# Scaling each token row twice: one buffer per tile, filled with gaps and scaled in place, instead of separate load and output tiles

## The chip, the cores and the metric

The kernel runs on one core of a Trainium2 chip. The metric is device time in microseconds of one execution. A core has a tensor engine (PE, not used here), VectorE (DVE), ScalarE (ACT), GpSimd (POOL), a sync engine (SP) that only waits and issues, and sixteen DMA engines that move data between the chip's main memory (HBM) and the on-chip memory (SBUF, 128 partitions). A DMA is issued from an engine's queue; here SP and ACT issue all of them.

## The reference

```python
batch, seq, hidden, n_experts = 16, 1024, 512, 8      # k = 2
def reference(x, expert_indices, expert_weights):
    x_expanded = x[:, :, np.newaxis, :].repeat(k, axis=2)
    weights = expert_weights[..., np.newaxis]
    return (x_expanded * weights).astype(np.float32)
```

Every token row of 512 float32 values (2 KB) is multiplied by two scalars, and both products are stored next to each other. The expert indices are not used. There are 16,384 tokens: 33.6 MB of x and 0.13 MB of weights are read, 67.1 MB are written. Each value that is read takes part in two multiplications.

## The kernel before, in words

The tokens are laid out over the 128 partitions so that each partition owns 128 consecutive tokens (`A_TOTAL`, L25). In the memory of x, the 128 tokens of a partition are one contiguous run, and so are their output rows. All weights are loaded first, as one tile `w_tile` of 1 KB per partition (L44, on SP's queue).

The main loop (L60) runs 16 times over blocks of 8 tokens per partition. `issue_load` (L48 to L55) allots one of three x tiles (16 KB per partition) and loads it by two DMAs on ACT's queue, four tokens (8 KB per partition, 1 MB in all) each. It is called two blocks ahead of the block that is computed. The block is then computed in two halves, each into its own output tile of 16 KB per partition (`o_tile`, L66, six buffers). A half is eight multiplications of a 128x512 operand by a scalar per partition: in the first half all eight are done by ScalarE (L79), in the second half six by ScalarE, one by VectorE and one by GpSimd (L85). Each finished half is stored by one DMA of 2 MB on SP's queue (L93), 16 KB contiguous in each partition on both sides.

What sets the order: each engine runs its own instructions in program order. On ACT's queue the two load DMAs of block `it + 2` stand in front of the multiplications of block `it`, so a load is issued when ScalarE has got through the block before, and waits there if the x tile that it will overwrite is still being read. Semaphores, put in by the framework, make a multiplication wait for its load and for a free output tile, a store wait for its multiplications, and a load wait for the readers of its tile. On SP's queue the stores follow each other in order.

Of the kernel before, what the change touches and what calls it, by code (L numbers as in the profile page):

```python
# [1 line left out]

# [4 lines left out]


@with_exitstack
def kernel(  # L10
    ctx: ExitStack,
    tc: tile.TileContext,
    x: bass.AP,
    expert_indices: bass.AP,
    expert_weights: bass.AP,
    out: bass.AP,
):
    nc = tc.nc

    batch, seq, hidden = x.shape  # L20
    k = expert_weights.shape[-1]
    P = nc.NUM_PARTITIONS
    ntok = batch * seq
    assert ntok % P == 0
    A_TOTAL = ntok // P  # L25

    xr = x.rearrange("b s h -> (b s) h").rearrange("(p a) h -> p a h", a=A_TOTAL)
    outr = out.rearrange("b s k h -> (b s) (k h)").rearrange(
        "(p a) n -> p a n", a=A_TOTAL
    )  # L30
    wr = expert_weights.rearrange("b s k -> (b s) k").rearrange(
        "(p a) k -> p a k", a=A_TOTAL
    )

    A = 8
    H = A // 2
    n_iters = A_TOTAL // A

    w_pool = ctx.enter_context(tc.tile_pool(name="w_pool", bufs=1))
    x_pool = ctx.enter_context(tc.tile_pool(name="x_pool", bufs=3))  # L40
    o_pool = ctx.enter_context(tc.tile_pool(name="o_pool", bufs=6))

    w_tile = w_pool.tile([P, A_TOTAL, k], mybir.dt.float32)
    nc.sync.dma_start(out=w_tile, in_=wr)  # L44

    x_tiles = {}

    def issue_load(j):  # L48
        if j >= n_iters:
            return  # L50
        t = x_pool.tile([P, A, hidden], mybir.dt.float32)
        a0 = j * A
        nc.scalar.dma_start(out=t[:, 0:H, :], in_=xr[:, a0 : a0 + H, :])
        nc.scalar.dma_start(out=t[:, H:A, :], in_=xr[:, a0 + H : a0 + A, :])
        x_tiles[j] = t  # L55

    issue_load(0)
    issue_load(1)

    for it in range(n_iters):  # L60
        a0 = it * A
        issue_load(it + 2)
        x_tile = x_tiles.pop(it)

        for half in range(2):
            o_tile = o_pool.tile([P, H, k, hidden], mybir.dt.float32)  # L66
            base = half * H
            opc = 0
            for ai in range(base, base + H):
                for kk in range(k):  # L70
                    w_ap = w_tile[:, a0 + ai, kk : kk + 1]
                    eng = nc.scalar
                    if half == 1:
                        if opc == 0 or opc == 8:
                            eng = nc.vector
                        elif opc == 4:
                            eng = nc.gpsimd
                    if eng is nc.scalar:
                        nc.scalar.mul(  # L79
                            out=o_tile[:, ai - base, kk, :],  # L80
                            in_=x_tile[:, ai, :],
                            mul=w_ap,
                        )
                    else:
                        eng.tensor_scalar(  # L85
                            out=o_tile[:, ai - base, kk, :],
                            in0=x_tile[:, ai, :],
                            scalar1=w_ap,
                            scalar2=None,
                            op0=mybir.AluOpType.mult,  # L90
                        )
                    opc += 1
            nc.sync.dma_start(  # L93
                out=outr[:, a0 + base : a0 + base + H, :], in_=o_tile
            )


# [1 line left out]
_INS = ['x', 'expert_indices', 'expert_weights']  # L99
_OUTS = [((16, 1024, 2, 512), 'float32')]  # L100


# [23 lines left out]
```

## Time and profile before

| what | before |
|---|---|
| time, three runs | 243.03 us median (242.64 to 245.35) |
| profiled execution, from its first to its last instruction | 243.2 us |
| moved by DMA in that span | 100.82 MB, mean 415 GB/s |
| store DMAs (SP's queue) | 32 of 2 MB, median 26.1 us from issue to landing |
| load DMAs (ACT's queue) | 32 of 1 MB, median 28.8 us from issue to landing |
| ScalarE multiplications | 224, mean 710 ns |
| VectorE multiplications | 16, mean 486 ns |
| GpSimd multiplications | 16, mean 1858 ns |

The page gives no time for the profiled execution other than its span; at 243.2 us it stands 0.2 us above the median of the three runs.

How to read the views that follow: in a line of a wait, the numbers are the time waited in total, how often, and the longest one, in us; "SPq" is the sync engine's own queue, which issues the stores. In a table by stage each line is a stretch of the span, its length, the busy time of each engine in it with the number of instructions, the tensor clock, the mean busy share of the sixteen DMA engines and what they moved in GB/s. A DMA line gives packets, MB and the share of the time of sixteen engines that these packets took. A DMA is cut into packets[...].

### The profile page before, as it was taken

To read this page: it belongs to the slowest core of one execution; us is meant where nothing else is said; L and a number is where in the kernel's file an instruction comes from. 1 tells how busy PE (TensorE), PEld (TensorE's weight loads), DVE (VectorE), ACT (ScalarE), POOL (GpSimd) and SP (SyncE) were. 2 spreads that over 40 slices of the span, in tenths; PEclk is the share of its full clock that TensorE was granted. 3 is DMA by queue.
4 is the path that set the end of the run, shared out by engine and by line. 5 is a ranking of instruction groups with operands and counts; after the bars stand their busy time and mean duration, and the time that the engine had idled before them with its cause. 6 is when DMAs were issued, how large, how long until landed. Compare 5 with 4: busy or idle time off the path is not lost.

```text
span 243.2 us, 500 instructions
## 1 busy us (share of the span) xinstructions
DVE 7.8 (3%) x16; ACT 140.3 (58%) x225; POOL 29.9 (12%) x20
## 2 busy tenths in 40 slices
DVE  0000000000000000000000000000000000000000
ACT  1999863909367291864909549094580996463000
POOL 0330303002030200303003030030301103020000
DMA  7999999999999999999999999999999999999991
GB/s 263 428 358 423 435 430 426 438 422 430 438 419 435 434 418 433 430 423 437 427 426 435 422 433 434 423 431 438 423 428 437 419 428 442 420 438 433 431 431 65
DMA packets 9363, 100.82 MB, mean 415 GB/s; under 512 B 1040, under 2 KB 1168, under 8 KB 1168
## 3 DMA queue, kind: packets, MB, share of 16 engines
q1 hardware_dynamic: 4752, 67.24, 64.8%
q10 hardware_dynamic: 4608, 33.56, 33.2%
q14 instruction: 3, 0.02, 0.0%
HBM read 33.69 MB, written 67.11 MB: 414 GB/s over the span
## 4 chain that ended last, share of the span: by engine, by line
DMA 83%; ACT 3%; ACTq 0%; issue 0%
DMA t<-in_x_dram 83%; ACT o_tile L79 3%; ACTq L121 0%; ACTq L79 0%
## 5 line engine op out<-in xcount | busy, mean ns | idle before, releaser
L79 ACT ACTIVATE o_tile<-t,w_tile 128x512 f32<-128x512 f32 x224 | 139.0, 710 | 75.7 <-DMA t<-in_x_dram 74.3
L85 POOL TENSOR_SCALAR o_tile<-t,w_tile 128x512 f32<-128x512 f32 x16 | 29.7, 1858 | 189.2 <-DMA t<-in_x_dram 189.2
L85 DVE TENSOR_SCALAR o_tile<-t,w_tile 128x512 f32<-128x512 f32 x16 | 7.8, 486 | 210.2 <-DMA t<-in_x_dram 210.2
L79 ACT ACT_TABLE_LOAD x1 | 1.3, 1283 | 5.3 <-DMA w_tile<-in_expert_weights_dram 5.3
L110 POOL MEMSET const-float32-0.0<- 128x1 f32 x1 | 0.1, 99 | 0.2 <-issue 0.2
L110 POOL MEMSET const-bfloat16-1.0<- 128x1 bf16 x1 | 0.1, 102 | 0.0
L110 POOL MEMSET const-uint8-127<- 128x1 uint8 x1 | 0.1, 102 | 0.0
L110 POOL MEMSET const-float32-1.0<- 128x1 f32 x1 | 0.1, 99 | 0.0
## 6 DMA issues: line engine op xcount, KB each, us to landing
out_dram<-o_tile SPq DMA_DIRECT2D x32, 2048.0 KB, 26.1
t<-in_x_dram ACTq DMA_DIRECT2D x32, 1024.0 KB, 28.8
w_tile<-in_expert_weights_dram SPq DMA_DIRECT2D x1, 128.0 KB, 4.5
```

Of the source, the lines that this page charges most:

```text
L79: nc.scalar.mul(out=o_tile[:, ai - base, kk, :], in_=x_tile[:, ai, :], mul=w_ap,)
L85: eng.tensor_scalar(out=o_tile[:, ai - base, kk, :], in0=x_tile[:, ai, :], scalar1=w_ap, scalar2=None, op0=mybir.AluOpType.mult,)
L110: nc = _bacc.Bacc("TRN2", target_bir_lowering=False, num_devices=1)
```

## The change

The separate load and output tiles go. There is one pool of six slots of 32 KB per partition; a slot holds the output block of 8 tokens: 8 tokens, 2 copies, 512 values. The load DMA writes x straight into the copy 0 rows of the slot: it reads one run of 16 KB per partition and writes eight rows of 2 KB, with gaps of 2 KB between them for copy 1. VectorE then makes all multiplications: for each token first copy 1 from copy 0 (`reversed`), then copy 0 in place. One DMA of 4 MB stores the slot, 32 KB contiguous per partition. There are 16 loads of 2 MB on ACT's queue and 16 stores on SP's queue. ScalarE and GpSimd compute nothing. A load into a slot waits until the store that last used the slot has landed; the first six loads wait for nothing. Nothing is issued ahead by hand; ACT's queue holds only the loads.

```diff
-    xr = x.rearrange("b s h -> (b s) h").rearrange("(p a) h -> p a h", a=A_TOTAL)
+    xr = x.rearrange("b s h -> (b s) h").rearrange("(p a) h -> p (a h)", a=A_TOTAL)
...
-    A = 8
-    H = A // 2
-    n_iters = A_TOTAL // A
+    T = 8
+    n_slots = A_TOTAL // T
...
-    x_pool = ctx.enter_context(tc.tile_pool(name="x_pool", bufs=3))
-    o_pool = ctx.enter_context(tc.tile_pool(name="o_pool", bufs=6))
+    pool = ctx.enter_context(tc.tile_pool(name="slots", bufs=6))
-    w_tile = w_pool.tile([P, A_TOTAL, k], mybir.dt.float32)
+    w_tile = w_pool.tile([P, A_TOTAL * k], f32)
     nc.sync.dma_start(out=w_tile, in_=wr)
...
+    for i in range(n_slots):
+        slot = pool.tile([P, T, k, hidden], f32)
+        nc.scalar.dma_start(
+            out=slot[:, :, 0, :],
+            in_=xr[:, i * T * hidden : (i + 1) * T * hidden],
+        )
+        for t in range(T):
+            for kk in reversed(range(k)):
+                c = (i * T + t) * k + kk
+                nc.vector.tensor_scalar(
+                    out=slot[:, t, kk, :],
+                    in0=slot[:, t, 0, :],
+                    scalar1=w_tile[:, c : c + 1],
+                    scalar2=None,
+                    op0=mybir.AluOpType.mult,
+                )
+        nc.sync.dma_start(
+            out=outr[:, i * T * row : (i + 1) * T * row], in_=slot
+        )
```

All other removed lines are `issue_load`, its calls and the loops over blocks and halves, which are printed above.

More of the change, by code (lines that the diff above doesn't have):

```diff
@@ L25 @@
     A_TOTAL = ntok // P
-    xr = x.rearrange("b s h -> (b s) h").rearrange("(p a) h -> p a h", a=A_TOTAL)
+    xr = x.rearrange("b s h -> (b s) h").rearrange("(p a) h -> p (a h)", a=A_TOTAL)
     outr = out.rearrange("b s k h -> (b s) (k h)").rearrange(
-        "(p a) n -> p a n", a=A_TOTAL
+        "(p a) n -> p (a n)", a=A_TOTAL
     )
     wr = expert_weights.rearrange("b s k -> (b s) k").rearrange(
-        "(p a) k -> p a k", a=A_TOTAL
+        "(p a) k -> p (a k)", a=A_TOTAL
     )
-    A = 8
@@ L36 @@
-    H = A // 2
-    n_iters = A_TOTAL // A
+    f32 = mybir.dt.float32
+    row = k * hidden
+    T = 8
+    n_slots = A_TOTAL // T
     w_pool = ctx.enter_context(tc.tile_pool(name="w_pool", bufs=1))
-    x_pool = ctx.enter_context(tc.tile_pool(name="x_pool", bufs=3))
-    o_pool = ctx.enter_context(tc.tile_pool(name="o_pool", bufs=6))
-    w_tile = w_pool.tile([P, A_TOTAL, k], mybir.dt.float32)
+    pool = ctx.enter_context(tc.tile_pool(name="slots", bufs=6))
+    w_tile = w_pool.tile([P, A_TOTAL * k], f32)
@@ L44 @@
     nc.sync.dma_start(out=w_tile, in_=wr)
[L46 to L95, printed above, removed]
```

## The prediction

> **What bounds the kernel now.** I read the page's busy lines first, then the DMA queues, the waits, and last a table by stage. The engines' line:
>
> ```profile
> DVE 7.8 (3%) x16; ACT 140.3 (58%) x225; POOL 29.9 (12%) x20
> ```
>
> No compute engine is busy for even 60% of the span of 243.2 us. The DMA queues, for the steady part from 20 to 200 us:
>
> ```profile
> DMA packets 7082, 77.25 MB, mean 429 GB/s; under 512 B 796, under 2 KB 796, under 8 KB 796
> ## 3 DMA queue, kind: packets, MB, share of 16 engines
> q1 hardware_dynamic: 3540, 51.50, 67.0%
> q10 hardware_dynamic: 3540, 25.73, 33.8%
> ```
>
> q1 carries the stores, q10 the loads. Together their packets took 100.8% of all sixteen DMA engines, so these are full. The 796 packets under 512 B are completion marks of 4 bytes. Of the others, a load packet has 8 KB (25.73 MB / 8192 = 3141 of them) and a store packet 16 KB (3143). The durations follow: a load packet takes 0.338 x 180 us x 16 / 3141 = 310 ns, a store packet 0.670 x 180 x 16 / 3143 = 614 ns. Two loads move as much as one store and take 620 ns, so a packet costs about **6 ns** beyond its bytes. Is anything outside the DMA engines late? The waits, of the engines and of the sync engine's queue:
>
> ```profile
> ACT o_tile L79 <- DMA t<-in_x_dram: 74.3, 14, 6.6
> ...
> SPq L121 <- DMA out_dram<-o_tile: 20.5, 2, 19.4
> ```
>
> ScalarE waits for loads; and when everything has been computed and issued, the queue still waits 19.4 us in one piece for stores to drain. Compute is hidden at both ends. By stage (us, DVE, ACT, POOL busy, clock, DMA share, GB/s):
>
> ```profile
> 6.00:12.00 6.00, 0.49 (x1) 5.99 (x10) 1.85 (x1) 1.00 1.01 429
> ...
> 14.00:16.00 2.00, 0.00 (x0) 1.86 (x4) 1.21 (x1) 1.00 0.99 250
> ...
> 110.00:160.00 50.00, 1.94 (x4) 27.72 (x45) 7.44 (x4) 1.00 1.01 428
> ...
> 219.00:236.00 17.00, 0.00 (x0) 2.23 (x4) 0.40 (x1) 1.00 1.01 431
> 236.00:238.00 2.00, 0.00 (x0) 0.00 (x0) 0.00 (x0) 1.00 0.86 369
> 238.00:240.00 2.00, 0.00 (x0) 0.00 (x0) 0.00 (x0) 1.00 0.12 49
> 240.00:242.00 2.00, 0.00 (x0) 0.00 (x0) 0.00 (x0) 1.00 0.06 25
> ```
>
> Loads alone, both mixed, and stores alone all run at 428 to 431 GB/s. There are three losses: nothing moves in the first 1.9 us; a dip at 14 to 16 us where stores join (2 us x (430 - 250)/430 = 0.8 us); and an uneven end. One engine's share is 431/16 = 27 GB/s, so from 240 to 242 us exactly **one of sixteen engines** is still working. In the completion events of the trace it is under 1 us behind the middle one until 80 us and 3.8 us behind from 200 us on; it sets the end.
>
> [...] The first microseconds show it:
>
> ```profile
> DMA packets 238, 0.97 MB, mean 314 GB/s; under 512 B 7, under 2 KB 135, under 8 KB 135
> ...
> q10 hardware_dynamic: 103, 0.84, 74.5%
> q1 hardware_dynamic: 135, 0.13, 17.3%
> ```
>
> From 1.5 to 4.6 us the weights' 128 rows of 1 KB (8 for an engine) went out beside 103 load packets of 8 KB: about one to one, **by count and not by bytes**. Eight pairs cost 8 x (0.31 + 0.04) = 2.8 us, and the weights landed 4.5 us after their issue; as one batch they would have taken 0.3 us. [...] its rate is equal with ScalarE busy (429) and nearly idle (431).
>
> **The change part by part**, as differences against the profiled span of 243.2 us; the three runs' median is 243.03 (242.64 to 245.35), so 0.2 comes off at the end.
>
> *Scaling.* The 224 ScalarE, 16 GpSimd and 16 VectorE operations become 256 on VectorE, at 486 ns in this trace (each stands alone there). [...] its 6.29 MB take the DMA engines 14.6 us at 430 GB/s. Cost 0, covered by transfers; uncovered it would be one slot's time at either end. That it works in place adds no instruction.
>
> *Start.* DMA begins at 1.9 us as now. The first 2 MB are in at 8.3 us (the second half tile's landing now), plus 7.8: the first store goes at about 16 us instead of 11.6. The six loads, issued with no wait, are 12.6 MB = 29 us of work, so the engines have loads until the stores come. The dip stays. Cost 0.
>
> *Queues and waits.* A load of slot i+6 waits on ACT's queue for the landing of store i. Behind it stand only later loads, as ScalarE no longer computes; now, loads stand behind 14 ACTIVATEs. On SP's queue 16 stores wait for VectorE in place of 32 that wait for three engines; the weights go first as now. With turns of 16 KB to 32 KB, as 8 to 16 now, a slot leaves every 14.7 us. Store 0 lands at about 31 us, store 9 at 31 + 9 x 14.7 = 163. Then the last load is issued, behind some three others, and lands after 3.4 x 14.7 = 50 us at 213; it is computed by 221, while two stores of 9.7 us each (at 431 GB/s) are ahead of it or running. The tail stays covered by a few us. Cost 0; if that cover fails it is up to 7.8 us.
>
> *Stores.* 4096 packets of 16 KB become 2048 of 32 KB: 2048 x 6 ns / 16 engines = **-0.8 us**.
>
> *Loads.* Today 4096 x 310 / 16 = 79.4 us of each engine. The source is one run of 16 KB in each partition, the destination eight rows of 2 KB; no row of the trace shows such a transfer. If only reads count: 2048 x 614 / 16 = 78.6 (-0.8). If each 2 KB row costs what a packet does: (304/4 + 6) = 82 ns x 16384 / 16 = 84.0 (+4.6)[...]. I take 80.0, so **+0.6**, nearer the low end because reads stay whole.
>
> *The late engine.* It fell behind by 3 us while 2 x 24 transfers were issued and ended; these are halved. If its loss goes by transfers, 1.5 us are saved, if by bytes nothing; bounds +1 to -2.8. I take **-1.0**.
>
> Sum: 243.2 + 0.6 - 0.8 - 1.0 = 242.0, less 0.2: **241.8 us**, its own range 239.5 to 244.5.
>
> **Rivals.** (a) *Starved loads, slower.* If an engine's turn is one 2 KB write row and not one 16 KB read, turns are 2 KB to 32 KB: loads get 1/17 of the rate, 25 GB/s, for as long as any store is queued. All stores drain, then loads run alone, in bursts. The engines stay full until the last burst; behind it nothing covers the last scaling, some 1.8 to 7.8 us. For it: turns go by count. Against it: what an engine reads from HBM is still 16 KB. +4.6 - 0.8 + 5 = **252 us** with full row cost, 246 to 248 with cheap rows and a part of the cover. It decides from turns of about 8 KB down: at 8 to 32 loads get a fifth of the bytes where they need a third, so they fall behind at every store until the stores run out. (b) *Row cost alone.* Turns stay 1:2, but each row costs a packet's 6 ns, or reads are cut to 2 KB too, so that the change doesn't read whole runs: 4.6 - 0.8 - 0.5 = +3.3, **246.3 us** (245 to 251 if a row costs double). For it: 6 ns is what this trace shows. (c) *Full gain.* Rows free, late engine within 1 us: -0.8 - 0.8 - 2.8 = **238.6 us**. Against it: the cause of its lag isn't known. Below 237 there is nothing: 1.9 + 100.8 MB / 431 GB/s (233.9) + 1.2 to land and end.
>
> **Numbers.** Forecast 0.48, (a) 0.20, (b) 0.12, (c) 0.20. Under 239.3 lies half of (c), and nearly half of (a) over 250: 239.3 to 250 holds eight in ten. A measurement tells about 1% (240.6 to 245.5) from no change. Faster: (c) and a fifth of the forecast, 0.29; slower: (a) and most of (b), 0.30; the rest, 0.41, within.
>
> **What would show it.** Right: both queues busy from 20 to 200 us, loads at 140 to 145 GB/s beside stores at 285, DMA share 1.0, last load in at 205 to 215 us, over 20 us of stores after VectorE's last operation. Row cost: mixed rate under 425 GB/s, q10's share over 34%. Starved: stretches with only loads, others with only stores, and VectorE ending within 15 us of the span's end. Wrong from the start: a DMA share well under 1.0 between 20 and 200 us, or VectorE over 14 us a slot.

## The result and the profile after

| | before | after |
|---|---|---|
| time, median | 242.98 us (242.64 to 245.35, 4 runs) | 258.77 us (258.64 to 259.42, 4 runs) |
| ratio to before, 95% interval | | 1.0635 (1.0578 to 1.0691) |
| span of the profiled execution | 243.2 us | 257.1 us |
| time of that execution | not given | 258.83 us |
| DMA rate over the span | 415 GB/s | 392 GB/s |

The change makes the kernel 6.4% slower, where the forecast was no clear difference (241.8 us, range 239.3 to 250). The same bytes are moved. Now and then an execution of a kernel takes one to two per cent longer than its others (of the kernel before, 245.35 us beside 242.64 here, and 246.95 beside 242.35 in the runs beside the experiments); the ratios leave out those more than 1.5% above the fastest. The page's engine, packet and queue lines for the kernel after:

```profile
DVE 102.1 (40%) x256; POOL 0.2 (0%) x4
...
DMA packets 19090, 100.81 MB, mean 392 GB/s; under 512 B 528, under 2 KB 656, under 8 KB 17040
## 3 DMA queue, kind: packets, MB, share of 16 engines
q1 hardware_dynamic: 2448, 67.24, 61.7%
q10 hardware_dynamic: 16640, 33.56, 35.2%
```

VectorE is busy for 40% only, so it isn't the bound of the whole. The loads (q10) are 16,640 packets: 256 completion marks and 16,384 of 2 KB. The forecast had taken 2048 packets of 16 KB. Beside the stores, from 68 to 92 us, the queues of the kernel after read:

```profile
DMA packets 642, 10.16 MB, mean 423 GB/s; under 512 B 32, under 2 KB 32, under 8 KB 352
## 3 DMA queue, kind: packets, MB, share of 16 engines
q1 hardware_dynamic: 322, 9.50, 91.7%
q10 hardware_dynamic: 320, 0.66, 7.0%
```

Turns go by count: about as many load packets as store packets. But a load packet carries 2 KB and a store packet 32 KB, so the loads get 6.5% of the bytes (0.66 of 10.16 MB) and need a third. What follows is in the table by stage of the kernel after (stretch, its length, VectorE and GpSimd busy, clock, DMA share, GB/s):

```profile
18.90:48.00 29.10, 8.98 (x23) 0.00 (x0) 1.00 1.03 440
48.00:51.50 3.50, 0.00 (x0) 0.00 (x0) 1.00 0.81 267
51.50:64.60 13.10, 9.49 (x24) 0.00 (x0) 1.00 1.05 388
64.60:94.50 29.90, 9.69 (x25) 0.00 (x0) 1.00 1.03 438
94.50:97.00 2.50, 0.00 (x0) 0.00 (x0) 1.00 0.78 239
97.00:110.50 13.50, 9.73 (x25) 0.00 (x0) 1.00 1.05 386
...
203.50:235.00 31.50, 9.02 (x23) 0.00 (x0) 1.00 1.01 427
235.00:238.70 3.70, 0.00 (x0) 0.00 (x0) 1.00 0.42 159
238.70:246.00 7.30, 6.42 (x16) 0.00 (x0) 1.00 0.00 0
246.00:256.30 10.30, 0.00 (x0) 0.00 (x0) 1.00 0.95 407
```

The kernel swings. For some 30 us stores run and loads starve, until all scaled slots are stored (the first, fourth and seventh line). Then only loads run, for 13 us at 386 to 388 GB/s, until VectorE has a slot ready. This repeats five times. In the last swing nothing follows the last load: VectorE scales for 6.4 us while **no byte moves for 7.3 us**, and then the last 4 MB go out alone. The wait of the sync engine's queue for the stores at the end, 19.4 us before, is now

```profile
SPq L92 <- DMA out_dram<-slot: 10.6, 1, 10.6
```

which is just this one store. Against 430 GB/s throughout (234.4 us for 100.8 MB) the span of 257.1 us splits so: start 1.9; the loads alone, 17 us at 384 at the start and 53 us at 387 later, 1.8 + 5.3 = 7.1; the switches from stores to loads, each reckoned with the stretch of stores before it (some of these show more than 430), 2.5 for the first four together and 2.5 for the last; bare scaling 7.3; the last store alone 0.6; after it 0.8. These add up to 22.7 us. The same reckoning leaves 8.8 us in the profiled execution of before. One loss of before is gone: the sixteen engines' completions of the last store lie within 0.3 us. Lateness isn't gone altogether: the last load is done on the middle engine (the median of its sixteen completions) at 236.8 us and on the last one at 238.6, and VectorE starts only then.

### The profile page after: what moved, and what is told of

It reads as the page before. It is cut to its first block, busy times and chain, and to the rows that moved or that the text cites. A ratio compares the mean times of both kernels' runs of the same rounds, so it can differ in the third digit from the quotient of the medians.

```text
span 257.1 us, 372 instructions
## 1 busy us (share of the span) xinstructions
DVE 102.1 (40%) x256; POOL 0.2 (0%) x4
## 3 DMA queue, kind: packets, MB, share of 16 engines
q10 hardware_dynamic: 16640, 33.56, 35.2%
## 4 chain that ended last, share of the span: by engine, by line
DMA 56%; another core or an unknown queue 20%; DVE 17%; ACTq 2%; issue 0%; DVEq 0%
DMA slot<-in_x_dram 56%; DVE slot L57 17%; ACTq L50 2%; DVEq L92 0%; DVEq L57 0%
## 5 line engine op out<-in xcount | busy, mean ns | idle before, releaser
L57 DVE TENSOR_SCALAR slot<-slot,w_tile 128x512 f32<-128x512 f32 x256 | 102.1, 480 | 143.1 <-DMA slot<-in_x_dram 143.1
```

Source lines behind the costliest of these rows:

```text
L57: nc.vector.tensor_scalar(out=slot[:, t, kk, :], in0=slot[:, t, 0, :], scalar1=w_tile[:, c : c + 1], scalar2=None, op0=mybir.AluOpType.mult,)
```

## The experiments

The theory, S: two queues take turns packet by packet; a packet is one row; so loads starve, and the end lies bare. The rivals: R, rows of 2 KB cost too much in themselves; W, a load waits until a 4 MB store has landed, and six slots are too few for that. The median of before, run beside the experiments, was 242.7 to 242.9 us.

**Both directions in one queue.** By S a store and the loads then follow each other and take no turns.

```diff
-        nc.scalar.dma_start(
+        nc.sync.dma_start(            # load(j): six ahead, then load(i + 5) behind store i
             out=slot[:, :, 0, :],
```

> The changed kernel with its loads moved from ACT's queue to SP's, so that loads and stores go through one queue in the order of their issue; rows, packets and VectorE's work are as in the changed kernel. Theory S (two queues take turns by packet; a load packet is one 2 KB row, a store packet 32 KB, so loads starve while a store is queued, and the last scaling is left bare): starvation ends, loads come at 388 GB/s, stores at 431, 1.9 + 86.5 + 155.7 + 1.2 = 245.3 us of span, so a time of 245 to 249 us. Rival R (the loss is the 2 KB rows' own cost): the rows are still there, no gain, 256 to 262 us. Rival W (the loss is that a load waits until a 4 MB store has landed, with too few slots): the wait is the same, and stores now stand behind it in the queue, 257 to 270 us.

Measured: 251.23 us, ratio to before 1.0349 (1.0322 to 1.0376). The table by stage:

```profile
6.00:34.00 28.00, 24.39 (x62) 0.00 (x0) 1.00 1.05 388
...
206.00:243.00 37.00, 0.36 (x1) 0.00 (x0) 1.00 1.00 431
243.00:246.00 3.00, 0.00 (x0) 0.00 (x0) 1.00 0.48 208
246.00:248.90 2.90, 0.00 (x0) 0.00 (x0) 1.00 0.03 11
```

Stores and loads took no turns: from 6 to 34 us two stores were issued, but what moved was 10.86 MB in 5383 packets, 80 of them marks and the rest load packets of 2 KB. 7.5 us are won with rows, packets and slots unchanged; the end is covered by 37 us of stores at full rate. R and W fall as the whole cause. It is 2 us above the range that S gave: the last engine came 3.0 us after the middle one, which the sum had left out.

**Stores of 4 KB rows.** A gap after each token's 4 KB makes the turns 2 KB to 4 KB, one to two as before the change.

```diff
-        slot = pool.tile([P, T, k, hidden], f32)
+        slot = pool.tile([P, T, row + PAD], f32)      # PAD = 8
...
-            out=outr[:, i * T * row : (i + 1) * T * row], in_=slot
+            out=outt[:, i * T : (i + 1) * T, :], in_=slot[:, :, 0:row]
```

> The changed kernel with a gap of 32 bytes after each token's 4 KB in the slot, so that a store reads rows of 4 KB in place of runs of 32 KB; loads as in the changed kernel. Theory S: turns are 2 KB to 4 KB, one to two as before the change; loads don't starve, the last load lands 20 us or more before the end. The rows cost: loads 16384 x 76 to 84 ns / 16, stores 16384 x 152 to 160 ns / 16: with start and end 238 to 254 us, I take 247. Rival R: shorter rows on both sides cost more, 262 us or more. Rival W: no change, 257 to 262 us.

Measured: 248.50 us, ratio 1.0238 (1.0222 to 1.0253). From 40 to 200 us:

```profile
DMA packets 22086, 66.79 MB, mean 417 GB/s; under 512 B 348, under 2 KB 348, under 8 KB 22085
## 3 DMA queue, kind: packets, MB, share of 16 engines
q1 hardware_dynamic: 11043, 44.53, 67.6%
q10 hardware_dynamic: 11042, 22.25, 35.7%
```

11,043 packets against 11,042: the turns couldn't be more even, and now the bytes stand as the work needs them. **Making the stores' rows shorter made the kernel 10 us faster**, which of the three only S gives. The price of short rows is the rate, 417 GB/s for the 429 of before.

**Stores of 8 KB rows.** The gap stands after every second token: turns of 2 KB to 8 KB. One thing more changes: a slot is loaded by two DMAs, the even and the odd tokens.

```diff
+        for u in range(G):                            # G = 2
+            nc.scalar.dma_start(
+                out=slot[:, :, u * row : u * row + hidden],
+                in_=xt[:, a0 : a0 + T // G, u, :],
+            )
...
+            out=outt[:, a0 : a0 + T // G, :], in_=slot[:, :, 0 : G * row],
```

> As the kernel with 4 KB store rows (248.5 us), but with the gap after every second token, so that a store reads rows of 8 KB; the loads are written in rows of 2 KB as there, by two DMAs a slot (even tokens, odd tokens). Theory S: turns are 2 KB to 8 KB, loads get a fifth of the bytes and need a third, so they fall behind, the stores run dry in stretches, and the last scaling lies bare: slower than with 4 KB rows although the rows are longer, 249.5 to 255 us, VectorE's last operation under 20 us before the end. Rival R (row cost alone decides): 8192 packets of 310 ns for 16384 of 158 are 3 us less, 244 to 247 us.

Measured: 251.51 us, ratio 1.0356 (1.0341 to 1.0372), 3.0 us slower than with 4 KB rows although the rows are longer. S holds and R falls. The two DMAs a slot don't explain it: alone at the start, from 6 to 12 us, the loads run at 396 GB/s, and at 395 with 4 KB rows. Stretches with loads alone are back; the second line is one (1514 load packets, one packet of the stores' queue), the first is mixed (1026 packets of the loads' queue with 2.04 MB, 1025 of the stores' with 8.13 MB):

```profile
24.00:48.00 24.00, 6.51 (x16) 0.00 (x0) 1.00 1.02 424
54.00:62.00 8.00, 7.25 (x19) 0.00 (x0) 1.00 1.05 376
226.00:246.00 20.00, 3.26 (x8) 0.00 (x0) 1.00 1.01 428
```

The last line shows what S had too gloomy: VectorE does its last work (3.26 us in this stretch) under stores, the end isn't bare here. Of these stretches the one with loads alone has the lowest rate, 376 GB/s; the loss of this kernel was not split up further.

**The last slot stored in quarters.** Only the end of the changed kernel is touched.

```diff
+            if (t + 1) % part == 0:                   # part = T // 4 in the last slot
+                a = i * T + t + 1 - part
+                nc.sync.dma_start(out=outr[:, a * row : (a + part) * row], ...
```

> The changed kernel with its last slot stored by four DMAs of 1 MB, each as soon as its four... two tokens per partition are scaled, in place of one of 4 MB after all sixteen operations. Theory S with the tail bare: of the 7.4 us from the last load's landing to the first byte of the last store, 16 operations of 0.40 us, all but the first four operations' 1.6 us are covered: 4.8 us less, 253 to 255 us. Rivals R and W: the end is covered by other transfers, 258 to 260 us.

Measured: 254.71 us, ratio 1.0492 (1.0475 to 1.0510), 4.1 us less than the change for 4.8 expected. The bare end is real, and most of the expected saving came:

```profile
238.00:240.00 2.00, 0.99 (x3) 0.00 (x0) 1.00 0.01 5
240.00:242.00 2.00, 2.00 (x6) 0.00 (x0) 1.00 0.30 127
242.00:244.00 2.00, 2.00 (x6) 0.00 (x0) 1.00 0.97 397
```

The first quarter leaves while VectorE still scales the rest.

**The gaps alone undone.** x is loaded packed into the slot's upper half, and VectorE spreads it over the same slot. Slots, engine, queues and waits stay.

```diff
         nc.scalar.dma_start(
-            out=slot[:, :, 0, :],
+            out=flat[:, x0 : 2 * x0],                 # flat: the slot as one row; x0 = T * hidden
...
-                    in0=slot[:, t, 0, :],
+                    in0=flat[:, x0 + t * hidden : x0 + (t + 1) * hidden],
```

> The changed kernel with the gaps alone undone: one pool of six 32 KB slots, VectorE, loads of 2 MB on ACT's queue that wait for the landing of the 4 MB store six slots before, stores on SP's. But x is loaded packed, one 16 KB run into the upper half of the slot, and VectorE spreads it from there to the output rows of the same slot. Theory S: packets of 16 KB to 32 KB, loads get their third, nothing starves, VectorE is done over 15 us before the end; what is left is the late engines, as with separate tiles (250.0 us), so 241 to 251 us. Rival W (six slots, each held from its load until a 4 MB store has landed): nothing of that has changed, 256 to 260 us. Rival R (row cost alone): what rows cost in one queue, 251.2 - 246.4 = 5 us less, 253 to 255 us.

Measured: 249.47 us, ratio 1.0224 (1.0147 to 1.0300); the four runs lie between 245.95 and 249.68. W falls: with the same six slots and the same waits 9.3 us of the 15.8 are gone. R, which gave 253 to 255, falls too. From 30 to 200 us its queues stand at

```profile
q1 hardware_dynamic: 1658, 48.14, 66.8%
q10 hardware_dynamic: 1668, 24.20, 33.6%
```

even in count, two to one in bytes. But it isn't the kernel before: something else costs 6.6 us.

**Where the other 6.6 us lie.** The same with separate tiles came first:

```diff
+        xt = x_pool.tile([P, T, hidden], f32)         # four, and four slots
+        nc.scalar.dma_start(out=xt, in_=xr[:, i * T * hidden : (i + 1) * T * hidden])
...
-                    in0=slot[:, t, 0, :],
+                    in0=xt[:, t, :],
```

> The changed kernel with the loads put into tiles of their own, packed as 16 KB runs on both sides (4 of 16 KB, and 4 output slots of 32 KB); VectorE does all scaling, loads are 2 MB on ACT's queue, stores 4 MB on SP's. Theory S: packets are 16 KB to 32 KB, loads get the third that they need, nothing starves: the time of the kernel before, 241 to 244.5 us; VectorE has done its last operation over 15 us before the end. Rival R: the same, 241 to 244.5. Rival W: fewer output slots, waits for 4 MB stores remain: over 250 us. Rival V (VectorE alone with 256 operations is what costs): over 252 us.

Measured: 249.97 us, ratio 1.0272 (1.0211 to 1.0333); S and R had given 241 to 244.5, W over 250 and V, a rival that blames VectorE's 256 operations, over 252. W comes within 0.03 us, but the end of the table by stage shows that no wait for a slot makes the time:

```profile
236.00:238.00 2.00, 0.00 (x0) 0.00 (x0) 1.00 0.87 377
238.00:240.00 2.00, 0.00 (x0) 0.00 (x0) 1.00 0.15 66
240.00:242.00 2.00, 0.00 (x0) 0.00 (x0) 1.00 0.15 66
242.00:244.00 2.00, 0.00 (x0) 0.00 (x0) 1.00 0.15 66
244.00:246.00 2.00, 0.00 (x0) 0.00 (x0) 1.00 0.08 33
```

The middle DMA engine is done with the last store at 238.8 us. From 238 to 244 us two or three of the sixteen are still working (66 GB/s is 2.4 shares of 27), and the last ends at 247.8, 9.0 us late. With all engines as fast as the middle one the span would end some 9 us earlier. In the packet records of this kernel single packets take up to 1 us more than the usual 611 or 1213 ns, mostly between 50 and 120 us and in the first 25. The kernel with the gaps undone in the slot ends the same way, its last engine 8.0 us behind the middle one.

Three more kernels asked what the lateness goes with. Packed loads, both directions in one queue:

```diff
-        nc.scalar.dma_start(
+        nc.sync.dma_start(                            # load(j): four ahead, then load(i + 4) behind store i
             out=xt, in_=xr[:, j * T * hidden : (j + 1) * T * hidden]
```

> Packed loads into tiles of their own (16 KB runs on both sides, four tiles) and 32 KB stores from four slots, VectorE scales, and both directions in SP's queue in the order load, store, load, store, with four loads ahead. Against the kernel with the rows of 2 KB in one queue (251.2 us) the rows alone are undone. Theory S: loads run at 430 and not 388 GB/s, 78 for 86.5 us, so 8 us less: 1.9 + 78 + 156 + 1.1 = 237 us of span, with a late engine of up to 3 us and some 2 us around the span 239 to 243 us. Against the packed loads on two queues (250.0), whose two late engines come 9 us behind: if lateness comes from two queues taking turns, it is gone here; if it comes from DMAs of 2 and 4 MB, it stays and the time is 245 to 251 us.

Measured: 246.44 us, ratio 1.0153 (1.0115 to 1.0191), 3.8 us late at the end, where S had given 239 to 243 us. So lateness doesn't need two queues, though with the same packets it is less than half of the 9.0 and 8.0 us there; whether taking turns adds to it stays open. Against the 251.23 us of the first experiment this is 4.8 us less, not 8, and the tiles and the number of loads ahead differ as well as the rows.

Half the size of DMA and packet on two queues, with everything on VectorE:

```diff
+    T = 4                                             # x tiles of 8 KB, slots of 16 KB, six each
```

> The packed loads on two queues (250.0 us, two late engines) with DMAs of half the size: loads of 1 MB in 8 KB runs into six tiles, stores of 2 MB in 16 KB runs from six tiles, as in the kernel before, but all scaling on VectorE. If VectorE's scaling costs nothing and the lateness of two engines there comes from the larger packets and DMAs: as before the change, 241 to 244 us. If VectorE's work is what delays two engines, or two queues on their own: 247 to 252 us.

Measured: 245.68 us, or 244.90 without one run of 249.47, ratio 1.0069 (1.0043 to 1.0096), between the two answers; 3.85 us late. These are the sizes of the kernel before, which with ScalarE is about 2 us faster.

Long DMAs, but gaps in both tiles, so that packets are 4 KB and 8 KB:

```diff
+        xt = x_pool.tile([P, T // G, G * hidden + PAD], f32)     # G = 2, PAD = 8
+        slot = pool.tile([P, T // G, G * row + PAD], f32)
```

> The packed loads on two queues with separate tiles (250.0 us, two engines 9 us late), same DMAs of 2 and 4 MB, but with a gap of 32 bytes after every second token in both tiles, so that load packets are 4 KB and store packets 8 KB, one to two as before. In the kernel with 2 KB and 4 KB packets no engine came late by over 1 us. If lateness goes with long packets: gone or under 2 us here, rate between 417 and 430 GB/s, 1.9 + 238 + 1 to 2 + 1.1 + 1.9 around the span = 242 to 246 us. If it goes with DMAs of 2 and 4 MB: two late engines again, 247 to 252 us.

Measured: 244.97 us, ratio 1.0086 (1.0069 to 1.0104), 1.2 us late, with the same DMAs of 2 and 4 MB as the kernel that is 9 us late. So on two queues lateness goes with long packets and not with long DMAs.

**Versions that might have beaten both.** The packed loads in the slot, with twelve half slots and with twenty-four quarter slots:

```diff
-    T = 8
+    T = 4                                             # the second: T = 2
...
-    pool = ctx.enter_context(tc.tile_pool(name="slots", bufs=6))
+    pool = ctx.enter_context(tc.tile_pool(name="slots", bufs=12))     # the second: bufs=24
```

> As the kernel with packed loads in the slot, with twelve slots of 16 KB: loads of 1 MB in 8 KB runs, stores of 2 MB in 16 KB runs, as in the kernel before. Theory S: nothing starves; late engines as with separate tiles of this size (245.7 us), so 241 to 247 us. If slots in place cost anything of their own: over 248 us.

> As the kernel with packed loads in twelve half slots (245.0 us), with twenty-four slots of 8 KB: loads of 0.5 MB in 4 KB runs, stores of 1 MB in 8 KB runs. If late engines go with long packets and long DMAs, under 1.5 us of lateness and a rate of 424 to 428 GB/s: 1.9 + 236.5 + 1.2 + 1.1 + 1.9 = 241 to 244 us, so at best level with the kernel before. If the shorter packets' own cost or 128 issues outweigh that: 245 to 249 us.

Measured: 244.97 us, ratio 1.0074 (1.0044 to 1.0103), and 245.79 us, ratio 1.0128 (1.0108 to 1.0149). The last engine is 1.7 us late in the one, 1.0 us in the other, whose rate is 423 GB/s for the 429 of before: what shorter packets save in lateness they lose in rate. None is faster than the kernel before.

| load and store packet, two queues | kernel | last engine behind the middle one, us | rate from 20 to 200 us, GB/s |
|---|---|---|---|
| 16 and 32 KB | separate tiles; in the slot | 9.0; 8.0 | 426; 425 |
| 8 and 16 KB | before; separate tiles; in the slot | 3.8; 3.85; 1.7 | 429; 426; 428 |
| 4 and 8 KB | separate tiles; in the slot | 1.2; 1.0 | 424; 423 |
| 2 and 4 KB | rows with gaps | 1.0 | 417 |

The lateness is that of one profiled execution each, and it varies: the other runs of before have spans of 240.6 to 241.2 us, some 2.3 us under the profiled one, and the profiled execution with 1.7 us (243.44 us) is the fastest of its six. With the gaps undone in the slot, 8.0 us against 3.8 covers 4.2 of the 6.6 us; if those 2.3 us are lateness too, it covers 6.5. That is an estimate, as the other executions were not traced.

## Why the prediction was wrong

**What bounds the kernel** held but for the bare end: the DMA engines do, before and after. VectorE's scaling took 6.4 us a slot, less than the 7.8 that 16 operations at the 486 ns of before come to; that is 0.40 us an operation back to back. That no higher rate than 431 GB/s was to be had, as the lower bound of 237 us assumed, was an estimate from the rates of before, 428 to 431.

**The step that failed** is "With turns of 16 KB to 32 KB, as 8 to 16 now, a slot leaves every 14.7 us". It put queues and waits at no cost; by the split above the bare end took 7.3 us and the switches 5.0. The turns by count had been read off the first microseconds and held. Wrong was what a load packet is. I took it for the 16 KB read and gave starvation 0.20, "what an engine reads from HBM is still 16 KB". It isn't: in the program as built, the load's source pattern is 128 x 8 x 512 values like its destination (strides 65536, 512 and 1), so both sides are cut into runs of 2 KB, and the trace has the 16,384 packets of that size. This could have been read from the built program beforehand. So the change does not do what its description says, one read of 16 KB; I had named that possibility, but under rival (b), as row cost only, and not joined it to the turns. With it, turns are 2 KB to 32 KB, and rival (a) follows from the prediction's own reading. Whether a transfer with whole reads and split writes would keep turns of 16 KB wasn't tried.

**Rival (a)** named the mechanism, the bursts and the bare end, and gave 252 us for 258.8. Of its terms, the bare end was put at 5 us and is 7.3; the rows at +4.6 and the loads alone lose 7.1; the switches, 5.0 us, were in no sum. Against these stands the late engine, 3.8 us in before, which that sum had kept. Beside the stores no cost of the rows shows: the five stretches run at 427 to 444 GB/s.

**Loads.** A 2 KB packet was bounded by 82 ns. Loads alone at 388 GB/s are 2048 / (388/16) = 84 ns, just above the bound: 8 ns beyond the 76 for the bytes, where the bound had 6.

**Start** held: the first store was issued at 15.2 us, forecast 16.

**Stores and the late engine.** A store packet of 32 KB takes 1213 ns where two of 16 KB took 2 x 611: 9 ns less, 1.2 us over the kernel for the 0.8 taken. The lateness at the end vanished, more than the 1.0 us taken, but for another reason, so the sign was luck: for 7.3 us no transfer runs, and then one store starts on all sixteen engines together. With the starvation gone it was 1.0 us with packets of 2 and 4 KB, but 8 to 9 us with those of 16 and 32 KB that the forecast had assumed. The bounds "+1 to -2.8" on that term were far too tight on the upper side, and the halving of transfers that I argued from isn't what it goes with: packets of twice the length made it worse. So the forecast of 241.8 us would most likely have missed even with whole 16 KB packets; the kernel with the gaps undone has them and takes 249.5.

**The 0.2 us taken off at the end** was wrong too: spans lie 1.7 to 2.1 us below the times of their runs (257.1 and 258.83; 240.7 and 242.72), so the profiled execution of before, at a span of 243.2, took some 245.3, most likely the 245.35 of the four runs. As the forecast only adds differences to the median, its number hardly changes.

## What to carry to other kernels

Where two queues share the DMA engines, compare the bytes of one contiguous row on each, as the built program cuts it: here the queue with rows of 2 KB beside 32 KB got 6.5% of the bytes for as long as the other had work, and it needed a third. A gap on the SBUF side alone cut the transfers of these kernels into packets of 2, 4 or 8 KB, where the other side was contiguous: the loads of the changed kernel into 16,384 of 2 KB, the stores with 4 KB rows into 11,043 for 44.53 MB, marks included, those with 8 KB rows into 1025 for 8.13 MB. If loads must be in short rows, bring the stores to the ratio that the work needs, or put both directions in one queue, and see what covers the last tile's compute. Here these two gave 248.5 and 251.2 us; packed loads, without short rows, gave 245.0 at best, so nothing tried was faster than the kernel before.

## What the runs showed of the hardware

- Two queues that both have work get equally many packets, at every pair of sizes looked at: 11,043 and 11,042 at 4 and 2 KB, 1658 and 1668 at 32 and 16 KB, 1025 and 1026 at 8 and 2 KB, 322 and 320 at 32 and 2 KB.
- Loads in 2 KB packets alone run at 376 to 396 GB/s, mostly 386 to 388, against 429 in 8 KB packets; beside 32 KB stores, at 427 to 444 GB/s, no cost of theirs shows.
- With packets of 16 and 32 KB on two queues single DMA engines fall behind by 8 to 9 us in 240, on one queue by 3.8; with 4 and 8 KB by 1.0 to 1.2. Why one or two engines take longer on some packets, and why ScalarE's version at 8 and 16 KB loses less than VectorE's, stays open: the trace shows the longer packets, not their cause.
